# A decoder block whose engine queues are sorted by the scheduler's timeline simulation

## The chip, the cores and the metric

The kernel runs on one core of a Trainium2 chip. A core has five engines, each with a queue of its own that is fixed when the program is built: TensorE (PE; its weight loads are shown apart, as PEld), VectorE (DVE), ScalarE (ACT), GpSimd (POOL) and SyncE (SP), which issues most of the transfers between HBM and the on-chip memory. Engines wait for one another through semaphores. The metric is the time of one execution on the device in microseconds (us); for each kernel the median of several runs is given.

## The reference

One layer on 512 tokens of width 1024, all in float32:

```
mod = silu(c) @ w_ada + b_ada        # shift, scale, gate for both halves
h = rmsnorm(x) * (1 + scale1) + shift1
x_rnn, q_lat, kv_lat, k_rope, g_rnn, g_mla = split(h @ w_in)
xc = causal_dwconv(x_rnn)            # 4 taps, 1280 channels
y_rnn = rg_lru(xc)                   # two gates, a linear recurrence over tokens
q, k, v = ...                        # 16 heads from the two latents, rotary part
y_mla = causal softmax attention     # 16 heads, 64 + 32 wide
merged = sigmoid(g_rnn) * (y_rnn @ w_proj_rnn) + sigmoid(g_mla) * (y_mla @ w_proj_mla)
x = x + gate1 * (merged @ w_out)
h2 = rmsnorm(x) * (1 + scale2) + shift2
u = causal_dwconv(h2 @ w_up)         # 3 taps, 2 x 2816 channels
x = x + gate2 * ((silu(u_gate) * u_val) @ w_down)
return rmsnorm(x)
```

## The kernel before

Activations stand with channels on the 128 partitions and the 512 tokens along the free axis, so that most products give a 128x512 tile in one PSUM bank. A float32 product is made of three matmuls in a reduced format: each operand is split in a high part (ACT, L133) and a low part (DVE, L134), and high times high, high times low and low times high are summed in PSUM (L165 to L167; in the token-major products L704 to L706). A weight is loaded by a transfer of 512 KB into one of three buffers called raw (L154), split into one of two buffers each of whl and whg, and used by TensorE; so every weight passes through a transfer, ACT and DVE before TensorE can take it, and a raw buffer comes free when DVE has split it.

The eight PSUM banks are shared out by tag: tr has three, acc three, fil and gm one each. The stages are:

- Start: x is loaded, its row sums of squares are taken, the modulation vectors of the first half are computed on DVE (L327), x is transposed (L351) and scaled to h, called A in the trace, and the latents for attention are projected.
- Attention, 16 heads: a head's scores go to the three acc banks (L573 to L575); DVE adds the mask and takes the maximum (L578), ACT takes the exponential (L585), TensorE transposes the result P (L595) into tr banks, ACT and DVE split it as pt, and TensorE multiplies it by V (L608). The projections of q, k and v for the next heads use the bank fil (evacuated at L516/L517 and L559/L560; the rotary step is L487 to L498). Between these stand the projections for the two output gates, which have long been ready to run and are given a low priority, as filling (function fill); their bank is mostly gm. DVE also computes the second half's modulation here (L629).
- Recurrence, ten tiles of 128 channels: projection into a tr bank, convolution (L724, L726), two gate products into acc banks, a chain of some twelve steps on ACT and DVE (L734 to L746), the scan over tokens (L747), and the split into yr. At its start DVE normalises the attention output Y (L770) and splits it as yhl. Eight projections of the attention output (L779), which use the banks fil and gm, fill in.
- Merge: the recurrence output is projected (eight tiles, ten chunks each, tr banks), gated and split again.
- Out stage: the product with w_out, token-major. Its first half of the channels goes to four banks at once; the second half is done for one tile of 128 tokens after another, t = 0 to 3, in the banks gm, fil, gm, fil. For each tile DVE multiplies by the gate and adds the residual (L822, L823), ACT sums the squares (L855), a few one-column steps give the norm's factor (L225 to L233), DVE scales the tile as R (L857), TensorE transposes it (L862), ACT and DVE apply scale and shift (L867, L869) and split it (L871, L872) as A, the input of the FFN.
- FFN: 44 projections of eight chunks each, the convolution (L898, L900), the gate, the product with w_down, the last norm and the output. Its first four weight tiles are split ahead into the ff and whl/whg buffers, and their products are done for the first 256 tokens ahead of the rest.

The order of the work is not written out. The kernel's functions issue instructions in program order, with priorities (tc.high_priority with an offset, such as AHR for the recurrence's projections or -LOW for the filling ones) and in some places a fixed chain (tc.issue_after, through in_order). From these, the dependencies and the buffers, the scheduler sets one static queue per engine when the program is built. The semaphores follow from the queues and the dependencies.

## Time and profile before

| | us |
|---|---|
| median of 3 runs | 892.94 (892.58 to 895.51) |
| the profiled execution | 893.23 |
| its span in the trace | 891.4 |

The profiled execution lies 0.3 us over the median, and 1.8 us of it lie outside the span. TensorE was granted 0.995 of its full clock. A row of a group or of the timeline names the line, engine and operation, then output<-inputs by the program's names; x is the count, the number in brackets the idle time before and what ended it. A matmul's end is modelled, and two that follow each other overlap in such rows.

### The profile page before, as it was taken

What the parts mean: (1) busy time and instruction counts of PE and PEld (TensorE: products, weight loads), DVE (VectorE), ACT (ScalarE), POOL (GpSimd) and SP (SyncE); (2) the same over time, 40 slices, a digit from 0 to 9 for tenths busy, and PEclk for the clock granted to TensorE, in tenths of its full rate; (3) what the DMA queues carried; (4) which work ended last, traced back from release to release, by engine and by line L of the source; (5) the groups of instructions that cost most, each with busy time, mean ns of one, the idle gap of its engine ahead of it and who ended that gap; (6) DMA issues with size and microseconds to landing.
All of it is one profiled execution on the core that took longest, in us unless ns stands there. A gap on an engine that the chain in (4) does not pass through costs nothing.

```text
span 891.4 us, 11238 instructions
## 1 busy us (share of the span) xinstructions
PE 861.5 (97%) x4032; PEld 688.9 (77%) x4032; DVE 644.7 (72%) x1222; ACT 487.7 (55%) x898; POOL 18.8 (2%) x43
## 2 busy tenths in 40 slices
PE   6999999999999999999999999999999999999996
PEld 2777877877877777777878898888788888788885
DVE  6988888879866989998655779766766666423524
ACT  4566777667745888888334545444544444322323
POOL 0001000001020000000000000000000000000000
PEclk9999999999999999999999999999999999999998
DMA  9903232334463243354325074333233233333322
GB/s 356 353 33 105 73 105 95 98 119 144 143 175 108 97 142 125 135 160 171 118 71 166 1 263 142 114 94 93 80 94 94 93 94 95 95 94 95 95 71 95
DMA packets 33804, 109.08 MB, mean 122 GB/s; under 512 B 4290, under 2 KB 8002, under 8 KB 33748
## 3 DMA queue, kind: packets, MB, share of 16 engines
q1 hardware_dynamic: 32116, 103.60, 35.2%
q0 software_dynamic: 1632, 4.75, 2.3%
q8 instruction: 32, 0.52, 0.2%
q14 instruction: 24, 0.20, 0.1%
HBM read 103.59 MB, written 2.13 MB: 119 GB/s over the span
## 4 chain that ended last, share of the span: by engine, by line
PE 62%; ACT 3%; DVE 3%; DMA 2%; issue 1%; POOL 0%; ACTq 0%; DVEq 0%; POOLq 0%
PE acc L165 9%; PE acc L167 9%; PE acc L166 9%; PE tr L165 3%; PE tr L167 3%; PE tr L166 3%; PE acc L704 2%; PE acc L706 2%; PE acc L705 2%; PE tr L948 2%; PE tr L947 2%; PE tr L946 2%; PE gm L165 1%; PE fil L705 1%; PE fil L706 1%; PE fil L704 1%
## 5 line engine op out<-in xcount | busy, mean ns | idle before, releaser
L134 DVE TENSOR_TENSOR whg<-raw,whg 128x512 fp32r<-128x512 f32 x119 | 81.6, 688 | 84.0 <-ACT whg L133 83.8
L133 ACT ACTIVATE whl<-raw 128x512 fp32r<-128x512 f32 (+2 forms) x131 | 74.8, 576 | 112.1 <-PE acc L167 26.7
L133 ACT ACTIVATE whg<-raw 128x512 fp32r<-128x512 f32 x119 | 74.3, 627 | 108.0 <-PE acc L167 53.9
L134 DVE TENSOR_TENSOR whl<-raw,whl 128x512 fp32r<-128x512 f32 (+2 forms) x131 | 80.8, 621 | 52.6 <-ACT whl L133 52.2
L165 PE MATMUL acc<-A,whl 128*128 128x512 f32 x184 | 73.3, 399 | 0.0
L167 PE MATMUL acc<-A,whl 128*128 128x512 f32 x184 | 72.9, 396 | 0.0
L166 PE MATMUL acc<-A,whl 128*128 128x512 f32 x184 | 72.5, 394 | 0.0
L167 PE MATMUL acc<-A,whg 128*128 128x512 f32 x176 | 70.2, 399 | 0.1
L165 PE MATMUL acc<-A,whg 128*128 128x512 f32 x176 | 70.0, 398 | 0.3 <-ACT whg L133 0.3
L166 PE MATMUL acc<-A,whg 128*128 128x512 f32 x176 | 69.2, 393 | 0.0
L900 DVE SCALAR_TENSOR_TENSOR Y<-acc,vec,Y 128x511 f32<-128x511 f32 x86 | 64.3, 748 | 1.3
L585 ACT ACTIVATE P<-P,mx,qsc 128x512 f32<-128x512 f32 (+1 forms) x64 | 41.3, 648 | 7.1 <-DVE mx L581 7.1
L165 PEld LDWEIGHTS acc<-A,whl 128*128 128x128 f32 x184 | 34.6, 188 | 8.6 <-issue 0.5
L166 PEld LDWEIGHTS acc<-A,whl 128*128 128x128 f32 x184 | 34.6, 188 | 8.3
L167 PEld LDWEIGHTS acc<-A,whl 128*128 128x128 f32 x184 | 34.5, 188 | 8.3
L165 PE MATMUL gm<-A,whg 128*128 128x512 f32 x96 | 38.9, 406 | 1.7 <-ACT R L408 1.2
L165 PEld LDWEIGHTS acc<-A,whg 128*128 128x128 f32 x176 | 33.0, 188 | 9.1 <-ACT whg L133 1.4
L167 PEld LDWEIGHTS acc<-A,whg 128*128 128x128 f32 x176 | 33.0, 188 | 8.8 <-DVE whg L134 0.7
L166 PEld LDWEIGHTS acc<-A,whg 128*128 128x128 f32 x176 | 33.0, 188 | 8.0
L167 PE MATMUL gm<-A,whg 128*128 128x512 f32 x96 | 38.6, 402 | 0.0
L166 PE MATMUL gm<-A,whg 128*128 128x512 f32 x96 | 38.1, 397 | 0.0
L898 ACT ACTIVATE Y<-acc,vec 128x512 f32<-128x512 f32 x43 | 32.9, 764 | 5.1 <-PE acc L167 5.1
(493 smaller groups left out, 2236.5 us busy)
## 6 DMA issues: line engine op xcount, KB each, us to landing
raw<-in_w_up SPq DMA_DIRECT2D x44, 512.0 KB, 3.5
raw<-in_w_dn SPq DMA_DIRECT2D x22, 512.0 KB, 3.5
wa<-in_w_adat SPq DMA_DIRECT2D x16, 512.0 KB, 9.0
raw<-in_w_adat SPq DMA_DIRECT2D x16, 512.0 KB, 3.3
raw<-in_w_xr SPq DMA_DIRECT2D x10, 512.0 KB, 4.1
raw<-in_w_pr SPq DMA_DIRECT2D x10, 512.0 KB, 3.7
raw<-in_w_gm SPq DMA_DIRECT2D x8, 512.0 KB, 5.5
raw<-in_w_gr SPq DMA_DIRECT2D x8, 512.0 KB, 4.1
```

The lines of the kernel that those rows point to most:

```text
L133: S.activation(h, src, AF.Copy)
L134: return V.tensor_tensor(dst[:, 1, lo_c:lo_c + n], src, h.bitcast(F32), SUB).ins
L165: PE.matmul(out, wh, x[:, 0, xs], start=start, stop=False)
L166: PE.matmul(out, wh, x[:, 1, xs], start=False, stop=False)
L167: return PE.matmul(out, wl, x[:, 0, xs], start=False, stop=stop).ins
L585: S.activation(pq, pq, AF.Exp, scale=qsc[:, qb:qb + 1], bias=mx[:, qb:qb + 1], accum_out=sm[:, qb:qb + 1])
L704: PE.matmul(out, lt[:, 0, s], w[:, 0, :], start=start, stop=False)
L705: PE.matmul(out, lt[:, 0, s], w[:, 1, :], start=False, stop=False)
L706: return PE.matmul(out, lt[:, 1, s], w[:, 0, :], start=False, stop=stop).ins
L898: S.activation(u, b, AF.Identity, scale=vc("fw", 2 * 2 * NF + cj), bias=vc("fb", cj))
L900: V.scalar_tensor_tensor(u[:, d:], b[:, :T - d], vc("fw", (2 - d) * 2 * NF + cj), u[:, d:], MUL, ADD)
L946: PE.matmul(b, lt[:, 0, s], w[:, 0, o:o + n], start=start, stop=False)
```

## The change

The tile scheduler is told to sort the engines' queues by a timeline simulation of its own in place of its default order:

```diff
-    with _tile.TileContext(nc) as tc:
+    with _tile.TileContext(nc, schedule_with_timeline_sim=True) as tc:
```

The instructions, their operands, the buffers and the priorities that the kernel asks for are the same; what differs is where each instruction stands in its engine's queue, and with it the waits. TensorE's, DVE's and ACT's queues differ from the start of the program to the end of the out stage; in the FFN they are almost the same. In SP's queue eight loads of the first modulation move behind six other loads, and a few loads change places later.

In the rows below, the names are those of the tiles (tag and a number), output<-inputs and the shape of the output, with xN for a repeated row.

The first place is DVE's queue at the end of the out stage. T_4227 holds the residual sums of token tiles 2 and 3, T_4226 those of tiles 0 and 1; gm_4541 and fil_4603 are the banks of tiles 2 and 3; R_4506 is the scaled tile 1, rs_4512 its factor; ff_* are split FFN weights. Before:

```order
L226 TENSOR_SCALAR rs_4510<-ssq_4508,s_4361 128x1
L227 RECIPROCAL rs_4512<-rs_4511 128x1
L229 SCALAR_TENSOR_TENSOR rs_4510<-rs_4510,rs_4512 128x1
L233 SCALAR_TENSOR_TENSOR rs_4512<-rs_4510,rs_4512 128x1
L857 TENSOR_SCALAR R_4506<-T_4226,rs_4512 128x1024
L822 TENSOR_TENSOR T_4227<-gm_4541,acc_2781 128x512
L823 TENSOR_TENSOR T_4227<-T_4227,Y_4221 128x512
```

With the change:

```order
L822 TENSOR_TENSOR T_4227<-fil_4603,acc_2781 128x512
L872 TENSOR_TENSOR A_4384<-R_4445,A_4384 128x4x128
L823 TENSOR_TENSOR T_4227<-T_4227,Y_4221 128x512
L872 TENSOR_TENSOR A_4384<-R_4445,A_4384 128x4x128
L227 RECIPROCAL rs_4512<-rs_4511 128x1
L823 TENSOR_TENSOR T_4227<-T_4227,Y_4221 128x512
L134 TENSOR_TENSOR ff_4675<-raw_4673,ff_4675 128x512
L134 TENSOR_TENSOR ff_4690<-raw_4673,ff_4690 128x512
L134 TENSOR_TENSOR ff_4707<-raw_4705,ff_4707 128x512
L134 TENSOR_TENSOR ff_4722<-raw_4705,ff_4722 128x512
L229 SCALAR_TENSOR_TENSOR rs_4510<-rs_4510,rs_4512 128x1
L134 TENSOR_TENSOR ff_4739<-raw_4737,ff_4739 128x512
```

One more ff split and the step L233 follow, and then L857, which writes R_4506. The scale of tile 1 has moved from ahead of the residual sum of tile 2 to behind those of tiles 2 and 3 and six weight splits.

The same place in ACT's queue, where rs_4511 is tile 1's root and tr_4519 holds its first four transposes. Before:

```order
L225 ACTIVATE rs_4511<-ssq_4508,s_4361 128x1
L867 ACTIVATE R_4507<-tr_4519,B_522,A_521 128x128 x4
L855 ACTIVATE R_4568,ssq_4570<-T_4227 128x512
L871 ACTIVATE A_4384<-R_4507 128x4x128 x2
L225 ACTIVATE rs_4573<-ssq_4570,s_4362 128x1
L133 ACTIVATE ff_4675<-raw_4673 128x512
```

With the change:

```order
L225 ACTIVATE rs_4511<-ssq_4508,s_4361 128x1
L133 ACTIVATE ff_4675<-raw_4673 128x512
L133 ACTIVATE ff_4690<-raw_4673 128x512
L133 ACTIVATE ff_4707<-raw_4705 128x512
L133 ACTIVATE ff_4722<-raw_4705 128x512
L133 ACTIVATE ff_4739<-raw_4737 128x512
L133 ACTIVATE ff_4754<-raw_4737 128x512
L133 ACTIVATE whl_4771<-raw_4769 128x512
L133 ACTIVATE whg_4786<-raw_4769 128x512
L133 ACTIVATE whl_4927<-raw_4925 128x512
L133 ACTIVATE whg_4930<-raw_4925 128x512
L867 ACTIVATE R_4507<-tr_4519,B_522,A_521 128x128 x4
```

Ten weight splits now stand ahead of the step that reads tile 1's transposes. In TensorE's queue those transposes (L862) follow the last matmul into fil_4603, and the FFN's first matmul follows them; before, they stood 22 matmuls ahead of the end of fil_4603.

The last place is TensorE's queue around an attention head with few other matmuls, P_1578 being its exponentials, pt_* their split transposes, v_* its V, fil_1634 a projection of k. Before:

```order
L595 MATMUL tr_1617<-ident,P_1578 128x128 x2
L165 MATMUL gm_1295<-A_89,whg_1298 128x512
L575 MATMUL acc_1693<-kt_737,q_1212 128x128
L165 MATMUL fil_1634<-kvn_727,whl_1637 128x512
L166 MATMUL fil_1634<-kvn_727,whl_1637 128x512
L167 MATMUL fil_1634<-kvn_727,whl_1637 128x512
L165 MATMUL fil_1634<-kvn_731,whl_1637 128x512
L166 MATMUL fil_1634<-kvn_731,whl_1637 128x512
L167 MATMUL fil_1634<-kvn_731,whl_1637 128x512
L608 MATMUL tr_1623<-pt_1602,v_1361 128x512 x2
```

With the change:

```order
L595 MATMUL tr_1601<-ident,P_1578 128x128 x4
L595 MATMUL tr_1609<-ident,P_1578 128x128 x4
L595 MATMUL tr_1617<-ident,P_1578 128x128 x2
L608 MATMUL tr_1623<-pt_1602,v_1361 128x512 x2
L608 MATMUL tr_1623<-pt_1610,v_1361 128x384 x2
L608 MATMUL tr_1623<-pt_1618,v_1362 128x256 x2
L608 MATMUL tr_1623<-pt_1610,v_1362 128x128 x2
```

The products with V follow the transposes directly; the other matmuls stand elsewhere, in longer runs into one bank.

## The prediction

> **What bounds the kernel now.** I read the page first, then the busy time by stage, then TensorE's waits. The page's head says that TensorE is the engine to watch, with VectorE next:

> ```profile
> span 891.4 us, 11238 instructions
> PE 861.5 (97%) x4032; PEld 688.9 (77%) x4032; DVE 644.7 (72%) x1222; ACT 487.7 (55%) x898; POOL 18.8 (2%) x43
> ```

> The share of 72% is an average over stages that differ. By stage (from the left: window, its length, then busy time of PE, PEld, DVE, ACT, POOL):

> ```profile
> core 0: us, PE busy (x) PEld busy (x) DVE busy (x) ACT busy (x) POOL busy (x), PEclk, DMA share, GB/s
> 95.00:255.00 160.00, 153.85 (x858) 126.97 (x857) 135.91 (x331) 114.80 (x274) 7.34 (x14) 1.00 0.36 113
> 255.00:425.00 170.00, 165.26 (x690) 125.77 (x689) 146.35 (x227) 128.59 (x196) 4.71 (x8) 1.00 0.44 141
> 425.00:536.00 111.00, 109.44 (x580) 92.26 (x579) 72.70 (x137) 49.13 (x98) 0.96 (x1) 1.00 0.38 126
> 536.00:891.40 355.40, 348.13 (x1558) 282.74 (x1557) 211.88 (x331) 141.00 (x236) 0.00 (x0) 0.99 0.31 95
> ```

> In attention (95 to 255 us) DVE is busy for 135.91 of 160 us, in the recurrence (255 to 425) for 146.35 of 170: 85 and 86%. There an order of DVE's queue that puts one item late has about 24 us of slack in a whole stage to make it good. In the FFN (from 536) DVE is at 60%, and the change hardly moves anything there. So only what lies before 536 us is at stake. Last, whom TensorE waits for (total, times, longest):

> ```profile
> PE tr L249 <- DVE crow L246: 3.9, 1, 3.9
> PE gm L257 <- POOL mask L198: 2.4, 1, 2.4
> PE gm L165 <- ACT R L408: 1.9, 2, 1.2
> PE tr L165 <- ACT q L133: 1.3, 1, 1.3
> PE acc L165 <- ACT A L871: 0.6, 1, 0.6
> PE tr L862 <- DVE R L857: 0.6, 1, 0.6
> ```

> Of these rows the first two are the start; I put all of TensorE's waits together at about 23 us, 8 of them in the first 15 us. This is what a better order could win at most: TensorE does the same matmuls in any order.

> **The change, part by part.** No instruction is added or removed; each engine's static queue is sorted anew. A queue runs in its order, so I cost the change by queues: for a piece of DVE's or ACT's new queue that begins with an instruction reading a PSUM bank which TensorE has just finished, and ends with one whose output TensorE needs next, I add up the durations of the piece and compare them with TensorE's matmuls between the two. What is over is a hole in TensorE. The work of a DVE instruction counts from start to start, some 0.07 us under its duration; a 128x512 matmul counts 0.23 us, since pairs start that far apart while each lasts 0.39.

> *Out stage, t = 1.* The scale that makes R_4506 (L857) is moved behind the residual sum of the last tile, fil_4603, which TensorE completes only with the last matmul of the stage. The rows of before for what now lies between:

> ```profile
> 508.43 0.75 DVE L857 TENSOR_SCALAR R<-T,rs 128x1024 f32<-128x1024 f32 x1
> 509.24 0.69 DVE L822 TENSOR_TENSOR T<-fil,acc 128x512 f32<-128x512 f32 x1
> 509.85 1.89 DVE L134 TENSOR_TENSOR ff<-raw,ff 128x512 fp32r<-128x512 f32 x3
> 515.34 0.68 DVE L872 TENSOR_TENSOR A<-R,A 128x512 fp32r<-128x512 f32 x1
> 515.94 0.68 DVE L823 TENSOR_TENSOR T<-T,Y 128x512 f32<-128x512 f32 x1
> ```

> From start to start 509.24 to 509.85 is 0.61 and 515.34 to 515.94 is 0.60. The new piece of DVE's queue, with L822 of gm_4541, which can itself only start a matmul earlier, is 2 L822, 2 L872, 2 L823 and 6 splits: 12 x 0.61 = 7.3, with L857 (0.75) and three one-column steps (about 0.3) 8.4 us. TensorE has one thing left meanwhile: the transposes of that R. It stands still for 8.4 us.

> Then ACT: the shift and scale of those transposes (L867) now stand behind ten weight splits. The last four read two transfers whose buffers come free only when DVE has split their former content, 4.9 and 6.1 us into the hole.

> ```profile
> raw<-in_w_up SPq DMA_DIRECT2D x44, 512.0 KB, 3.5
> 515.36 0.63 ACT L133 ACTIVATE whl<-raw 128x512 fp32r<-128x512 f32 x1 [0.48 <-DMA raw<-in_w_up]
> 521.96 1.50 ACT L867 ACTIVATE R<-tr,B,A 128x128 f32<-128x128 f32 x4 [2.65 <-PE tr L862]
> 523.50 1.15 ACT L871 ACTIVATE A<-R 128x512 fp32r<-128x512 f32 x2
> 524.18 0.62 PE L165 MATMUL acc<-A,ff 128*128 128x256 f32 x3 [0.62 <-ACT A L871]
> 521.29 1.07 PE L862 MATMUL tr<-ident,R 128*128 128x128 f32 x8 [0.59 <-DVE R L857]
> ```

> The second lands at 6.1 + 3.5 = 9.6; two splits (1.2) make 10.8, L867 12.3, an L855 of about 0.6 that now stands between 12.9, and half of L871 13.5. In these 13.5 us TensorE does the transposes, 1.07. **+12.4 us**; 11 if the splits of DVE start before the bank is read, 14 if a transfer takes a microsecond more.

> *The last recurrence tile (yr_3797).* Before, TensorE had matmuls of the MLA projection to do while the chain of this tile ran:

> ```profile
> 407.24 0.39 PE L167 MATMUL acc<-xh,whl 128*128 128x512 f32 x1
> 408.23 0.69 ACT L734 ACTIVATE pr<-acc,hba 128x512 f32<-128x512 f32 x1
> 414.53 1.28 ACT L743 ACT_TABLE_LOAD   x1
> 418.01 1.22 DVE L747 TENSOR_TENSOR_SCAN pr<-pr 128x512 f32<-128x512 f32 x1
> 419.27 0.63 ACT L133 ACTIVATE yr<-pr 128x512 fp32r<-128x512 f32 x1 [0.60 <-DVE pr L747]
> 419.96 0.73 PE L165 MATMUL tr<-yr,whl 128*128 128x512 f32 x2
> ```

> The gates end at 407.6, the split is there at 419.9: 12.3 us, some of it other work between. Bare, the chain is ten dependent steps of about 0.7 with the scan, the split and what the table load adds: 9.3. Now 19 matmuls stand between the last gate and the first use, 19 x 0.23 = 4.4, with the gate's own end 4.7. **+4.7 us**; 3.5 at 8.2 for the chain without the table load, 7.6 with the 12.3 of before.

> *Attention.* The filling gate projections now come in blocks of up to 24 matmuls, where they were strewn between the steps of a head, so that a head's scores, transposes and products with V follow one another with less between. And on DVE, several instructions of other heads now stand between a score bank and the split that its product waits for. The dearest piece begins with the maximum over acc_2021 and ends with the split of pt_2191. Its members by these rows:

> ```profile
> L578 DVE CUSTOM_DVE_ANT_0 P<-acc,mask 128x512 f32<-128x512 f32 x16 | 11.0, 686 | 0.2 <-PE acc L575 0.2
> L629 DVE CUSTOM_DVE_ANT_0 raw<-raw,crow,vec 128x1024 f32<-128x1024 f32 x16 | 20.5, 1281 | 2.8 <-DMA raw<-in_w_adat 2.8
> L517 DVE TENSOR_TENSOR q<-fil,q 64x512 fp32r<-64x512 f32 x16 | 11.0, 687 | 1.2 <-ACT q L516 1.0
> L134 DVE TENSOR_TENSOR pt<-tr,pt 128x512 fp32r<-128x512 f32 x32 | 20.9, 684 | 2.9 <-ACT pt L133 2.6
> ```

> Two L629 at 1.21, sixteen of full size at 0.61 (two L578, four L517, four pt, the five of the rotary step, L613), and nine narrower ones, 2.7 together: 14.9 us, say 15, against 8.6 us of matmuls: 6.4 over. Seven more pieces that don't overlap give 2.5, 1.2, 0.3, 1.6, 1.0, 3.0 and 2.5: 18.6 in all. The same reckoning on the old queues gives 7.9 here, 4.0 in the recurrence and 0.5 in the out stage, 12.4 together, where the trace has about 15 us of waits outside the start. So the reckoning is near, and low if anything. **Net +10.7 us** (half to one and a half times that).

> *Recurrence.* The worst piece stands at its start: from the first convolution step on tr_2804 to the low split of whl_2979, 29 DVE instructions, among them eight normalisations of Y and eight splits of the result:

> ```profile
> L770 DVE TENSOR_TENSOR Y<-Y,yr 128x512 f32<-128x512 f32 x8 | 5.2, 686 | 3.2 <-DMA yr<-rd 3.2
> L134 DVE TENSOR_TENSOR yhl<-Y,yhl 128x512 fp32r<-128x512 f32 x8 | 5.2, 688 | 0.3
> ```

> 29 at 0.61 are 17.7 us, against 43 matmuls, 9.9 us: 7.7 over. Before, all sixteen stand ahead of that first convolution step. Six further pieces give 3.6, 0.5, 2.5, 1.5, 1.3 and 0.5: 17.6 in all, less the 4.0 of before. **Net +13.6 us**, with the same bounds as in attention.

> *Start.* In SP's queue eight modulation loads (512 KB each) move behind cst, posi, three loads of w_gm and vec1. The transfers run close together here, and the matmuls that follow the latents are ready at about the same time: **+0.6 us**, from -0.9 to 2.1. On POOL only two memsets change places, before any use: nothing, and hidden under the loads of x.

> *The clock.* Where TensorE was idle for long, its next matmuls ran slowly. At the start, by rows:

> ```profile
> 8.38 3.78 PE L249 MATMUL tr<-crow,ones 128*128 128x512 f32 x4 [3.91 <-DVE crow L246]
> 18.46 3.17 PE L257 MATMUL gm<-mask,ones 128*128 128x512 f32 x6
> ```

> Four of one form take 0.95 each after the idle time, six of the same form 0.53 each when it has been working: 4 x 0.42 = 1.7 us per long hole. The out stage has two long holes (8.4, then about 4): **+3 us**; none at all is the lower end, five holes (8.5) the upper.

> [...]

> Sum: 12.4 + 4.7 + 10.7 + 13.6 + 0.6 + 3 = 45.0. The profiled execution took 893.23 us, 0.3 over the median, so **938 us** against 892.94.

> **The rivals.**

> *Only the two fixed holes* (12.4, 4.7) and the start. For it: in attention and recurrence DVE is idle for 24 us each, and could run ahead into TensorE's blocks of fill. Against it: the reckoning found the waits of before about right. 893.2 + 17.7 = 911 us.

> *More than I add up.* Each weight split that is late also frees its load buffer late, of which there are three, and the next transfer needs 3.5 us. If nine of the pieces that end in a weight split each brought one such transfer into view, 9 x 3.5 = 31: about 969 us. Against it: the DMA share of 0.36 and 0.44 leaves the transfers short.

> *Not slower.* The blocks of fill could keep TensorE fed past what it waits for now; the first wait, 3.9 on crow, may also shrink, since that product now stands ahead of the sums of squares on DVE. If all 23 us went, and of the new costs only the lower ends of the two fixed holes came (11 + 3.5), 893.2 - 23 + 14.5 = 885 us. It decides only if attention and recurrence cost nothing, and the hole after fil_4603 can't be escaped by any engine's running ahead, since it begins with TensorE's own last matmul. If the gain came to 15 it would be no change.

> **How the numbers follow.** My forecast has 0.75, the two holes alone 0.12, more than I add up 0.08, not slower 0.05 (faster 0.03, within 0.3% 0.02; 0.3%, 2.7 us, is about what a measurement of this kernel can tell from none). The forecast's own range, from the lower ends 11 + 3.5 + 12.2 - 0.9 = 25.8 to the upper ends 14 + 7.6 + 36.5 + 2.1 + 8.5 = 68.7, is 919 to 962; to hold eight in ten it reaches down towards the two holes alone: **910 to 962 us**. Slower: 0.75 + 0.12 + 0.08 = 0.95.

> **What would show it.** In the changed profile TensorE should wait for "DVE R L857" once for about 8 us and then for "ACT A L871" for about 4, around the end of the out stage; wait about 5 us for the split of yr; show waits of several us for DVE's pt, whl and whg splits between 95 and 430 us; and the stretch of the FFN should be as long as it was, 355 us. TensorE's busy time should hardly change. If the out stage has no such pair of waits, the queue argument is wrong; if it has, and the stages before are as long as they were, DVE ran ahead.

## The result and the profile after

The changed kernel takes 977.82 us (median; 976.90 to 982.99), the kernel before, timed beside it, 893.13 us: a ratio of 1.0955, with a 95% interval of 1.0912 to 1.0997. It is slower by 84.7 us, as forecast in sign, and by nearly twice the forecast 45; 977.82 lies outside 910 to 962. The profiled execution is the slowest of the four, 982.99 us, 5.2 over the median. One of the three executions of the kernel busy_after below ran at a lower granted clock than the others and took longer (1039.0 us at 0.838, the others 981.08 and 980.12 at 0.983 and 0.982), and is compared with nothing.

The head of the page of the changed kernel, to be laid beside the one of before:

```profile
span 981.2 us, 11235 instructions
PE 886.5 (90%) x4032; PEld 714.1 (73%) x4032; DVE 647.3 (66%) x1222; ACT 489.3 (50%) x898; POOL 18.7 (2%) x43
```

DVE and ACT do what they did, within 3 us. TensorE, with the same 4032 matmuls, is busy for 25.0 us more, and idle for 94.7 us instead of 29.9. The 89.8 us of the span are these two: 65 of waiting and 25 of slower matmuls.

Where they lie, by windows that end with the last product of attention with V, the last scan, and the start of the first FFN matmul. Before:

```profile
0.00:251.40 251.40, 236.30 (x1197) 186.40 (x1198) 212.34 (x528) 166.85 (x364) 12.61 (x33) 0.99 0.44 148
251.40:418.00 166.60, 161.02 (x676) 123.08 (x676) 141.20 (x219) 127.82 (x195) 5.20 (x9) 1.00 0.43 140
418.00:510.20 92.20, 91.47 (x405) 72.85 (x403) 58.35 (x106) 37.52 (x76) 0.00 (x0) 1.00 0.28 90
510.20:891.40 381.20, 372.73 (x1760) 306.60 (x1758) 232.76 (x370) 155.56 (x264) 0.96 (x1) 0.99 0.34 105
```

With the change (columns as in the prediction: window, length, busy time and count of PE, PEld, DVE, ACT, POOL, then the granted clock):

```profile
0.00:311.30 311.30, 270.84 (x1310) 217.94 (x1310) 219.60 (x539) 176.44 (x380) 12.57 (x33) 0.95 0.38 128
311.30:489.70 178.40, 149.49 (x573) 112.86 (x571) 137.78 (x211) 120.61 (x181) 5.19 (x9) 0.92 0.38 118
489.70:595.10 105.40, 90.01 (x386) 72.83 (x386) 60.86 (x107) 39.49 (x79) 0.95 (x1) 0.92 0.31 97
595.10:981.20 386.10, 376.12 (x1766) 310.52 (x1766) 229.10 (x365) 152.79 (x259) 0.00 (x0) 0.99 0.31 98
```

The lengths can't be subtracted as they stand, since matmuls have moved between the stages: 113 more are done by the end of attention, 103 fewer in the recurrence. At 0.23 us each:

| stage | longer by | matmuls moved in | lost |
|---|---|---|---|
| start and attention | 59.9 | +113, 26.0 us | 33.9 |
| recurrence | 11.8 | -103, -23.7 us | 35.5 |
| merge and out stage | 13.2 | -19, -4.4 us | 17.6 |
| FFN to the end | 4.9 | +6, 1.4 us | 3.5 |

They add up to 90.5 for 89.8. Attention has lost three times the 11.3 that the prediction gave it with the start, the recurrence twice its 18.3 (with yr), and the out stage about what it was given (15.4): 2.0 of its 17.6 are the end of the wait for yr, which falls into that window.

Whom TensorE waits for now:

```profile
PE tr L165 <- ACT whl L133: 18.4, 10, 3.1
PE tr L608 <- DVE pt L134: 9.2, 5, 3.7
PE tr L862 <- DVE R L857: 8.3, 1, 8.3
PE acc L165 <- ACT A L871: 7.0, 2, 5.2
PE tr L165 <- ACT yr L133: 5.1, 1, 5.1
PE tr L595 <- ACT P L585: 5.0, 3, 2.0
PE acc L165 <- ACT A L355: 4.5, 1, 4.5
```

Two of these rows before, where there is none for pt over 0.5:

```profile
PE tr L165 <- ACT whl L133: 1.1, 3, 0.5
PE tr L595 <- ACT P L585: 0.9, 3, 0.4
```

The rows of R, A and yr are the holes that the prediction named one by one. The largest is one that it did not have as a row of its own: ten waits of 0.7 to 3.1 us for the high split of a weight, on ACT, nine of them in the recurrence's projections. None of the waits in attention and recurrence, apart from that for yr, is longer than 3.7, so the single holes of 6.4 and 7.7 us that the prediction gave to these stages did not come as holes. The three named holes in TensorE's timeline:

```profile
491.66 1.22 PE L165 MATMUL tr<-yr,whl 128*128 128x512 f32 x2 [5.11 <-ACT yr L133]
...
588.04 1.94 PE L862 MATMUL tr<-ident,R 128*128 128x128 f32 x8 [8.31 <-DVE R L857]
595.14 1.01 PE L165 MATMUL acc<-A,ff 128*128 128x256 f32 x3 [5.16 <-ACT A L871]
```

And what stands behind one of the ten. The chain of waits of the changed kernel between 333 and 353 us (start, length, what; a piece that begins where the one above ends was released by it; pieces of 0.02 us between them, called issue, are left out):

```profile
333.89 3.49 DMA raw<-in_w_pm
337.40 0.64 ACT whg L133
338.06 1.29 DVE whg L134 x2
...
340.05 0.63 ACT xh L133
...
343.38 0.69 DVE pr L745
344.07 0.61 DVE whl L134
344.70 3.29 DMA raw<-in_w_ada
348.02 1.42 DVE acc L423 x2
349.43 0.67 DVE Y L737
350.13 0.73 ACT Y L738
...
352.22 0.53 ACT whl L133
352.79 0.80 PE tr L165
```

For 19 us TensorE is not in the chain at all. It goes from a transfer to ACT, to DVE, to ACT, back to DVE, which frees a load buffer (L134); into that buffer goes a transfer for the vector of the first gate (L419); its accumulation on DVE (L423) stands in the queue ahead of a step of the gates (L737), ACT's step after it stands ahead of the split of whl, and TensorE waits 3.11 us for that. No piece of one queue between two events of TensorE holds this sum.

### The profile page after: what moved, and what is told of

The parts are those of the page before. It is cut to its first block, busy times and chain, and to the rows that moved or that the text cites. A ratio compares the mean times of both kernels' runs of the same rounds, so it can differ in the third digit from the quotient of the medians.

```text
span 981.2 us, 11235 instructions
## 1 busy us (share of the span) xinstructions
PE 886.5 (90%) x4032; PEld 714.1 (73%) x4032; DVE 647.3 (66%) x1222; ACT 489.3 (50%) x898; POOL 18.7 (2%) x43
## 4 chain that ended last, share of the span: by engine, by line
PE 61%; DVE 11%; DMA 7%; ACT 7%; issue 2%; POOL 0%; DVEq 0%; ACTq 0%
PE acc L167 8%; PE acc L165 8%; PE acc L166 8%; PE tr L165 3%; PE tr L166 2%; PE tr L167 2%; PE acc L704 2%; PE acc L706 2%; PE acc L705 2%; DMA raw<-in_w_pm 2%; DMA raw<-in_w_adat 2%; PE fil L165 2%; PE tr L948 2%; PE tr L947 2%; PE tr L946 2%
## 5 line engine op out<-in xcount | busy, mean ns | idle before, releaser
L134 DVE TENSOR_TENSOR whg<-raw,whg 128x512 fp32r<-128x512 f32 x119 | 81.3, 689 | 102.7 <-ACT whg L133 102.5
L133 ACT ACTIVATE whl<-raw 128x512 fp32r<-128x512 f32 (+2 forms) x131 | 75.2, 575 | 131.3 <-issue 29.5
L133 ACT ACTIVATE whg<-raw 128x512 fp32r<-128x512 f32 x119 | 73.7, 628 | 124.1 <-PE acc L167 60.9
L134 DVE TENSOR_TENSOR whl<-raw,whl 128x512 fp32r<-128x512 f32 (+2 forms) x131 | 81.2, 621 | 52.2 <-ACT whl L133 51.9
L165 PE MATMUL acc<-A,whl 128*128 128x512 f32 x184 | 71.5, 399 | 5.4 <-ACT A L355 4.5
L167 PE MATMUL acc<-A,whl 128*128 128x512 f32 x184 | 73.8, 401 | 0.0
L167 PE MATMUL acc<-A,whg 128*128 128x512 f32 x176 | 70.1, 398 | 0.0
L165 PE MATMUL acc<-A,whg 128*128 128x512 f32 x176 | 69.4, 395 | 0.0
L900 DVE SCALAR_TENSOR_TENSOR Y<-acc,vec,Y 128x511 f32<-128x511 f32 (+1 forms) x86 | 64.1, 748 | 1.3
L165 PE MATMUL tr<-A,whl 128*128 128x512 f32 x80 | 35.1, 439 | 15.6 <-ACT whl L133 15.6
L165 PEld LDWEIGHTS acc<-A,whl 128*128 128x128 f32 x184 | 34.7, 190 | 14.0 <-ACT A L355 4.7
L165 PE MATMUL gm<-A,whg 128*128 128x512 f32 x96 | 39.0, 406 | 2.2 <-ACT whg L133 2.2
L167 PEld LDWEIGHTS acc<-A,whl 128*128 128x128 f32 x184 | 34.9, 190 | 7.9
L578 DVE CUSTOM_DVE_ANT_0 P<-acc,mask 128x256 f32<-128x256 f32 (+1 forms) x64 | 28.8, 484 | 17.9 <-PE acc L575 17.7
L165 PEld LDWEIGHTS acc<-A,whg 128*128 128x128 f32 x176 | 33.0, 188 | 8.2 <-issue 0.2
L167 PE MATMUL tr<-A,whl 128*128 128x512 f32 x80 | 35.1, 439 | 4.0 <-DVE whl L134 4.0
L167 PEld LDWEIGHTS acc<-A,whg 128*128 128x128 f32 x176 | 33.0, 188 | 7.7
## 6 DMA issues: line engine op xcount, KB each, us to landing
raw<-in_w_up SPq DMA_DIRECT2D x44, 512.0 KB, 3.5
raw<-in_w_dn SPq DMA_DIRECT2D x22, 512.0 KB, 3.6
wa<-in_w_adat SPq DMA_DIRECT2D x16, 512.0 KB, 9.0
raw<-in_w_adat SPq DMA_DIRECT2D x16, 512.0 KB, 3.2
raw<-in_w_xr SPq DMA_DIRECT2D x10, 512.0 KB, 3.5
raw<-in_w_pr SPq DMA_DIRECT2D x10, 512.0 KB, 3.5
raw<-in_w_gm SPq DMA_DIRECT2D x8, 512.0 KB, 5.2
raw<-in_w_gr SPq DMA_DIRECT2D x8, 512.0 KB, 3.8
```

Of the source, the lines that this page charges most:

```text
L133: S.activation(h, src, AF.Copy)
L134: return V.tensor_tensor(dst[:, 1, lo_c:lo_c + n], src, h.bitcast(F32), SUB).ins
L165: PE.matmul(out, wh, x[:, 0, xs], start=start, stop=False)
L167: return PE.matmul(out, wl, x[:, 0, xs], start=False, stop=stop).ins
L578: V.tensor_tensor_reduce(out=pt[:, POFF[qd]:POFF[qd] + n], in0=sc[qd], in1=mask[:, T - n:], scale=1.0, scalar=-3e38, op0=ADD, op1=ALU.max, ...
L900: V.scalar_tensor_tensor(u[:, d:], b[:, :T - d], vc("fw", (2 - d) * 2 * NF + cj), u[:, d:], MUL, ADD)
```

## The experiments

All kernels but the plain two are built with queues that are imposed: a table for an engine lists its instructions, and each is told to be issued behind the one ahead of it in the table. Such a link sets an order and adds no wait. An engine without a table is sorted by the default order around those that have one. The edit that all of them share:

```diff
+QUEUES = {'PE': ..., 'DVE': ..., 'Activation': ..., 'Pool': ..., 'SP': ...}
+def _queues(tc, nc, *engines):
+    traced = list(nc.cur_bb.bb.instructions)
+    for engine in engines:
+        q = ...
+        for i, j in zip(q[:-1], q[1:]):
+            tc.add_manual_dep(traced[j], traced[i].name, mybir.DependencyInfo(mybir.DependencyClass.NoSync, ...), reason="queue")
...
+        _queues(tc, nc, *QUEUES)
```

The whole tables of either kernel give that kernel's queues row by row. The diffs below show only what else differs. Each ratio is against the kernel before, on the same chip.

| kernel | us | ratio and interval | us over before |
|---|---|---|---|
| the change | 977.82 | 1.0955 (1.0912 to 1.0997) | 85 |
| busy_after | 981.08 | 1.0988 (1.0954 to 1.1022) | 88 |
| out_as_before | 962.34 | 1.0773 (1.0737 to 1.0810) | 70 |
| out_only | 908.07 | 1.0181 (1.0146 to 1.0215) | 16 |
| att_only | 950.65 | 1.0642 (1.0609 to 1.0676) | 59 |
| rnn_only | 929.53 | 1.0410 (1.0381 to 1.0440) | 38 |
| noload_after | 966.42 | 1.0839 (1.0790 to 1.0887) | 74 |
| noload_before | 889.30 | 0.9963 (0.9953 to 0.9973) | -3 |
| nomod_after | 961.73 | 1.0769 (1.0748 to 1.0791) | 69 |
| nomod_before | 888.35 | 0.9954 (0.9926 to 0.9983) | -5 |
| pe_only | 974.82 | 1.0916 (1.0873 to 1.0959) | 82 |
| dve_only | 1025.00 | 1.1478 (1.1448 to 1.1508) | 132 |
| dve_act_only | 1028.57 | 1.1528 (1.1494 to 1.1563) | 137 |
| fills_spread | 939.96 | 1.0538 (1.0489 to 1.0587) | 46 |
| heads_order | 917.99 | 1.0273 (1.0237 to 1.0310) | 24 |

### Is it the clock?

The mean granted clock fell from 0.995 to 0.954, and TensorE's busy time rose by 25 us. If that were on the path, filling the holes with idle work would give a part of it back. busy_after has all queues of the change, and 63 matmuls with zero weights in 16 of the longest holes:

```diff
+IDLE = {514: 5, 528: 4, 567: 2, ..., 1688: 12, 1712: 7}
+    def busy(out, start):
+        hook[0] += 1
+        n = out.shape[-1]
+        EXTRA.append([PE.matmul(out, mask[:, :P], mask[:, :n], start=start, stop=start).ins
+                      for _ in range(IDLE.get(hook[0], 0))])
...
+        busy(out, start)
         PE.matmul(out, wh, x[:, 0, xs], start=start, stop=False)
```

> The queues of the change, written out as a table and imposed, with 63 extra matmuls on TensorE (a zero weight, so they add nothing) placed in 16 of the holes that the changed kernel's trace shows, 60 to 70% of each hole's length, just ahead of the matmul that waits. Theory clock: about 20 to 25 us of the 85 are matmuls run at half clock after windows in which TensorE was busy for less than half of 3.4 us; with the holes filled the granted clock rises from 0.954 to 0.975 or more and the time falls by 8 to 18 us, to 960 to 970. Rival: the slow matmuls lie beside other waits and cost nothing; the time stays within 3 us of 978 or grows by up to 10.

Measured: 981.08 us at a granted clock of 0.983. Seven tenths of what the clock had lost are back (0.954 to 0.983, of 0.995), and no time is: the interval of the ratio overlaps that of the change. The likely reading is that most of the slow matmuls lie ahead of waits that end when another engine is done, where a faster matmul only waits longer. What the 63 matmuls cost where a hole had already closed is in the same number, at most 63 x 0.23 = 14.5 us, so a gain of some 12 us could be hidden; one of 17, seven tenths of 25, could not.

### Which stage?

out_only takes the order of the out stage and what follows from the change, all else from before; out_as_before is its counterpart. att_only and rnn_only take that of start and attention, and of the recurrence, from the change.

```diff
-QUEUES = {'PE': <the change's>, ...}
+QUEUES = {'PE': <before's, with the out stage's places filled in the change's order>, ...}      # out_only
+QUEUES = {'PE': <the change's, with the out stage's places filled in before's order>, ...}      # out_as_before
+QUEUES = {'PE0': <up to the end of attention, the change's>, 'PE1': <the rest, before's>, ...}  # att_only
+QUEUES = {'PE0': <attention, before's>, 'PE1': <recurrence, the change's>, 'PE2': <rest>, ...}  # rnn_only
```

> Only the out stage and the FFN in the order of the change, the rest exactly as before. The prediction's terms: 12.4 and about 3.4 for the clock over before, to about 908.5; the changed kernel without its out stage gave back 15.5 (977.8 to 962.3). If the three stages alone add up to less than 70, they make one another worse.

> The queues of the change imposed, except that all instructions of the out stage and the FFN stand among themselves in the order of before. Theory queues, by the prediction's out-stage term and the clock of two long holes: the time falls by 12.4 + 3.4, to about 962. Rival: the holes only hide other waits, which come up when they go; it falls by less than 6, to 972 or more.

> Start and attention (with the gate projections) in the order of the change, recurrence, merge, out stage and FFN in the order of before, each stage's order imposed on each engine and the default scheduler left to interleave the two. Theory queue sums, by the prediction's terms: 10.7 + 0.6 over before, to about 904. Rival, from the changed kernel's trace (25 us more TensorE idle time up to the end of attention, and half clock besides): 25 to 45 us over before, 918 to 938.

> Only the recurrence and merge in the order of the change, the rest as before, imposed in the same way. Theory queue sums: 13.6 + 4.7 over before, to about 911. Rival, from the changed trace (23 us more TensorE idle time there, and half clock besides): 23 to 35 us over before, 916 to 928.

Measured: out_only costs 16.1 us (908.07 - 891.96), as the prediction's terms say (908.5), and its waits are those that the queue sums named:

```profile
PE tr L862 <- DVE R L857: 8.3, 1, 8.3
PE acc L165 <- ACT A L871: 5.6, 2, 3.7
```

out_as_before gives back as much: 1.0955 - 1.0773 is 0.018, 16 us. The prediction had 12.4 for the stage and 3 for the clock after it, 15.4: this term was right. The 3.4 for the clock in two of the expectations is twice the 1.7 us a hole from the start's rows, not rounded.

att_only costs 58.7 us, more than either expectation, but its queues don't fit together where the two orders meet, just behind the attention:

```profile
PE tr L165 <- ACT whl L133: 19.9, 5, 16.6
```

Taking off that one wait of 16.6, which the change doesn't have, leaves 42 us. rnn_only costs 37.6, just over its rival's range. The three stages make 42 + 37.6 + 16.1 = 95.7 for 85, so they are not quite separate; but each of the two long stages costs far more by itself than its term in the prediction (11.3 and 18.3). So the excess needs no interplay of stages.

### Is it the transfers, or the modulation on DVE?

The chain above passes through a load for the first gate, which has a low priority, and its accumulation. noload leaves out 24 such loads, 16 for the second half's shift and scale and 8 for the first gate (the steps work on data that is there instead, so these three vectors are not the reference's); nomod leaves out the steps L629 and the first gate's L423 as well, and GpSimd sets the shift and scale to zero. Both were made of the change's queues and of before's.

```diff
-                    w = raw()
-                    dma(w, a["w_adat"][2 * NK + NK * e + k])
+                    w = crow
...
-                            V.tensor_tensor_reduce(out=w[:, c], in0=w[:, c], in1=crow[:, c], scale=0.5,
+                            V.tensor_tensor_reduce(out=w[:, c], in0=w[:, c], in1=crow[:, c], scale=0.0,
...
-            r = alloc()
-            dma(r, a["w_ada2"][sec, kk])
+            if sec == 0:
+                r = h[:, 0].rearrange("p e n -> p (e n)").bitcast(F32)
+            else:
+                r = alloc()
+                dma(r, a["w_ada2"][sec, kk])
```

For nomod, the loops themselves are cut:

```diff
-                for i in range(2):
+                for i in range(2 * sec):
                     c = slice(i * T, i * T + T)
                     V.scalar_tensor_tensor(acc[:, c], r[:, c], cact[:, kk:kk + 1], acc[:, c], MUL, ADD)
...
-                    w = raw()
-                    ...
-                            V.tensor_tensor_reduce(out=w[:, c], in0=w[:, c], in1=crow[:, c], scale=0.5,
-                            ...
```

> The queues of the change imposed, with the 24 loads (512 KB each) of modulation weights in attention and recurrence left out: DVE does the same steps at the same places in its queue, on tiles that are there already (so these modulation vectors are wrong), and the three load buffers serve the other weights alone. Theory transfers: the waits that the queue sums missed come from loads brought into view by the three buffers, which those late DVE steps hold; the time falls by 20 us or more, to 957 or less. Rival queues: the engines' order alone makes the holes; it falls by 6 us at most, what DVE itself waits for these loads.

> The queues of before imposed, with the same 24 loads left out in the same way. Both theories: the loads are hidden there; the time falls by 4 us at most, to 889 or more. If it falls as far as with the queues of the change, the loads cost as much in either order and say nothing of the change.

> The queues of the change imposed, with the 24 modulation loads and also the 32 DVE steps that use them (16 of L629 in attention, 16 of L423 in the recurrence) left out; these modulation vectors are wrong. Theory misplaced low-priority work: such steps stand in DVE's queue ahead of steps that a head or a recurrence tile waits for, and hold everything behind them; without them the time falls well under the 966 that leaving out the loads alone gave, to 930 or less. Rival chains: the order of the critical steps themselves makes the holes, through DVE and ACT in turn; it falls to 945 to 960, about the steps' own 31 us of DVE work that the chains pass through in part.

> The queues of before with the same loads and steps left out. Both theories: they are hidden there; 3 to 6 us under before, 886 to 889.

What counts is the distance between the two orders. With everything it is 0.0955, 85 us. Without the loads it is 1.0839 - 0.9963 = 0.0876, 78 us; without the steps too, 1.0769 - 0.9954 = 0.0815, 73 us. The transfers are 7 us of the loss, the modulation's work on DVE some 5 more; the intervals of the ratios are 1 to 5 us to either side, so both are small and neither is sure to a few us. With all of it gone, six sevenths of the loss stand. From the change's own 978, noload_after takes off 11, between what its two theories asked for (20 or more, 6 or less), and nomod_after ends just above the 945 to 960 of "chains", far from the 930 of "misplaced low-priority work". So these transfers are links in chains that would be nearly as late without them. Loads of other weights use the same three buffers and are still there, but with the 24 gone ACT and DVE wait only 7.6 us in all for loads into raw in attention and recurrence (29.3 in the change, 12.3 before), and 78 of the 85 us stand all the same.

### Which engine's queue?

The prediction was made from DVE's and ACT's queues. pe_only imposes TensorE's queue of the change, dve_only DVE's, dve_act_only DVE's and ACT's; the default order sorts the other engines around it.

```diff
-QUEUES = {'PE': ..., 'DVE': ..., 'Activation': ..., 'Pool': ..., 'SP': ...}
+QUEUES = {'PE': ...}                      # pe_only
+QUEUES = {'DVE': ...}                     # dve_only
+QUEUES = {'DVE': ..., 'Activation': ...}  # dve_act_only
```

> TensorE's queue as in the change, all others left to the default scheduler. DVE's and ACT's queues alone as in the change gave 1028.6. Theory: TensorE's order is not what costs; with DVE and ACT sorted to suit it the time is nearer before than the change, under 930 (the out stage keeps part of its hole, since the transposes stand last there, about 3 to 8 us). Rival: either half of the change alone costs as much as both, 960 or more.

> DVE's queue alone as in the change. Theory chains through DVE and ACT in turn: with ACT free to follow, part of the loss goes, 930 to 970. Rival: DVE's order alone carries it all, 1000 or more, since ACT's steps follow DVE's anyway.

> DVE's and ACT's queues as in the change, TensorE's, SP's and GpSimd's left to the default scheduler, which sorts them around these. Theory: the holes come from what DVE and ACT do first, and TensorE's order only follows; the time is within 15 us of the changed kernel's 978. Rival: TensorE's blocks of fill make the holes, by taking away what covered a head's steps; the time is nearer before, under 930.

Measured: TensorE's queue alone brings 82 us, as much as the whole change; DVE's alone brings 132, and DVE's with ACT's 137, more than either expectation for it. The theory that DVE's and ACT's order is at fault, and TensorE's would do no harm under the default order of the others, has fallen. So has the reverse, that the default order of TensorE heals the loss. TensorE's queue or DVE's, imposed alone, costs as much or more. My reading, which these runs don't show by themselves, is that each is half of a plan, and that a sort that did not make the plan doesn't fit the other half to it as well. In these runs the other engines' queues are neither those of before nor those of the change, since they are sorted anew around the imposed one; one queue of the change with all others word for word as before wasn't tried.

With TensorE's queue imposed, the waits are of another make-up but the same size. In pe_only:

```profile
PE tr L595 <- ACT P L585: 18.0, 10, 4.5
PE tr L165 <- ACT whl L133: 13.0, 9, 2.9
```

### What in TensorE's queue?

Two things differ in it: the filling matmuls stand in blocks, and the steps of the heads (scores, transposes, products with V) stand in another order, two heads close behind each other. fills_spread is pe_only with the filling matmuls strewn as before (102 runs of them, half of three or fewer) and the out stage as before. heads_order is TensorE's queue of before with only the heads' steps in the change's order. With TensorE's queue of before imposed and nothing else, the sort gives all engines the queues of before, row by row; in heads_order DVE's and ACT's queues differ from those inside attention alone.

```diff
-QUEUES = {'PE': <the change's>}
+QUEUES = {'PE': <fills in before's places, the rest in the change's order, from the out stage on before's>}  # fills_spread
+QUEUES = {'PE': <before's, with L573 to L575, L595 and L608 in the change's order>}                          # heads_order
```

> TensorE's queue imposed, the other engines left to the default scheduler: all of TensorE's instructions up to the out stage in the order of the change among themselves, but the 576 matmuls of the filling projections (gates in attention, MLA projection in the recurrence) in the queue's places where the order of before has them (102 runs, half of them 3 or shorter, where the change has 60, half of them 10 or longer); the out stage as before. Theory cover: TensorE's order costs because the filling comes in blocks and leaves a head's or a tile's steps bare; spread again, the time is under 915. Rival: the order of the other matmuls costs; with the 5 to 10 us of the out stage gone from 974.8, the time is 945 or more.

> TensorE's queue as before, the other engines left to the default scheduler, but scores, transposes and products with V of the 16 heads in the order of the change among themselves (in the places that these steps have before). Theory cover: the order of the head steps themselves matters little; within 10 us of before, under 903. Rival: heads in pairs, as the change has them, cost; 915 or more.

Measured: heads_order costs 24 us, with the rest of TensorE's queue as before. The window to the end of its attention:

```profile
0.00:277.20 277.20, 244.81 (x1197) 194.50 (x1198) 213.75 (x528) 167.52 (x364) 12.59 (x33) 0.95 0.40 134
```

That is 25.8 us more than the 251.40 of before, with the same 1197 matmuls; in the recurrence it loses nothing (its last scan ends 166.5 us later, for 166.6). The mechanism shows in the timeline, at the second head of a pair:

```profile
214.80 0.69 DVE L578 CUSTOM_DVE_ANT_0 P<-acc,mask 128x512 f32<-128x512 f32 x1
...
220.88 0.45 PE L608 MATMUL tr<-pt,v 128*128 128x384 f32 x2
...
223.64 0.15 DVE L581 TENSOR_TENSOR mx<-mx,nqsc 128x4 f32<-128x4 f32 x1
223.82 0.81 ACT L585 ACTIVATE P<-P,mx,qsc 128x512 f32<-128x512 f32 x1 [1.27 <-DVE mx L581]
226.53 0.90 PE L595 MATMUL tr<-ident,P 128*128 128x128 f32 x3 [5.20 <-ACT P L585]
```

The same head before:

```profile
202.19 0.69 DVE L578 CUSTOM_DVE_ANT_0 P<-acc,mask 128x512 f32<-128x512 f32 x1
...
208.22 0.75 PE L608 MATMUL tr<-pt,v 128*128 128x384 f32 x5
...
211.58 0.15 DVE L581 TENSOR_TENSOR mx<-mx,nqsc 128x4 f32<-128x4 f32 x1
...
216.03 1.31 PE L595 MATMUL tr<-ident,P 128*128 128x128 f32 x10 [0.44 <-ACT P L585]
```

In heads_order the maximum over its scores is done at 215.4, and the small product that turns it into the exponential's bias (L581, four columns, 0.15 us long) comes at 223.6, behind thirteen other steps of DVE's queue: one of the modulation (L629), five of the rotary step for another head, the splits of the first head's pt, of two weights and of two pieces of k. Only then does ACT start on the exponentials, one block after another (2.5 us), and TensorE, which has reached the end of its matmuls ahead of the transposes at 221.3, stands for 5.20. Before, the path is no shorter: the product comes 8.8 us after the maximum, behind fourteen steps, and the transposes follow at 216.0. But there 32 matmuls (20 of projections, 12 of the next head's scores) stand between the first head's last product and these transposes, and TensorE waits for 0.44. In heads_order these 32 come after the first transposes. A head's path between its scores and its transposes goes through DVE, ACT and back, and needs TensorE to have other work meanwhile; what the new order takes away is not a short path but the work that covered it. With two heads close behind each other, the second has none.

The change itself takes away cover in the same way at another step. Its longest wait in attention is at the head of P_1578, where the products with V now follow the transposes directly and the split of pt stands behind other steps of DVE:

```profile
182.88 2.61 PE L608 MATMUL tr<-pt,v 128*128 128x512 f32 x8 [3.68 <-DVE pt L134]
```

fills_spread costs 46 us where pe_only costs 82. In the recurrence, pe_only first:

```profile
305.70:490.00 184.30, 150.85 (x573) 113.63 (x571) 137.84 (x212) 120.52 (x181) 5.16 (x9) 0.90 0.37 114
```

and fills_spread:

```profile
275.50:464.20 188.70, 167.35 (x681) 127.16 (x680) 143.82 (x220) 129.18 (x196) 5.20 (x9) 0.98 0.40 126
```

Worked out as in the table of stages, pe_only loses 184.3 - 166.6 + 103 x 0.23 = 41.4 us there, fills_spread 188.7 - 166.6 - 5 x 0.23 = 20.9. In attention it is 54.3 - 113 x 0.23 = 28.3 (end at 305.7) and 24.1 - 3 x 0.23 = 23.4 (end at 275.5). So strewing the fills gives 5 us in attention and 20 in the recurrence; the other 10 of the 36 lie behind it, where fills_spread has the out stage of before. Its 940 us lie between the two expectations (under 915, 945 or more). TensorE's waits in fills_spread:

```profile
PE tr L595 <- ACT P L585: 12.5, 7, 4.9
PE tr L165 <- ACT whl L133: 8.9, 9, 1.9
```

The waits for whl shrink from 13.0 to 8.9, those for P from 18.0 to 12.5. In pe_only, then, the heads' order, which costs 25.8 us in attention by itself, is about the size of what attention loses (28.3), and the blocks of fill make about half of what the recurrence loses. The change's own queues lose 33.9 and 35.5 there; that the same two causes share these losses in the same way is inferred, not shown. The other 21 us of the recurrence come with the order of the remaining matmuls or with how DVE and ACT are sorted around it; which, no run here tells.

## Why the prediction was wrong in size

**The out stage (12.4, and 3 for the clock): right.** The hole at R was 8.31 for 8.4 and that at A 5.16 for about 4 (3.7 in out_only), and the stage alone cost 16.1 for 15.4. The piece that the prediction summed begins with TensorE's own last matmul, TensorE has nothing else to do, and only one queue at a time lies between: what the sum assumes holds there.

**The last recurrence tile (4.7): right**, 5.11.

**Attention (+10.7) and the start (+0.6): mis-sized by a factor of three**, 33.9 in place of 11.3. The step that failed is "for a piece of DVE's or ACT's new queue that begins with an instruction reading a PSUM bank ... and ends with one whose output TensorE needs next, I add up the durations of the piece". Such a piece sees one engine's queue. A head's path is DVE, ACT, TensorE, ACT and DVE again: the 8.2 us from a maximum to its small product in heads_order end with something that ACT needs, not TensorE, so no piece of the sum holds them. The path was as long before (8.8 us) and cost 0.44, for 32 matmuls covered it. What the prediction had to price was the cover that goes; it noted that a head's steps follow one another "with less between", and gave that change no price of its own. And its dearest piece, 6.4 us over, did not come as a hole: the longest wait of the stage is 3.68. In the start, the row of "ACT A L355", 4.5 us, was not foreseen.

**Recurrence (+13.6, with yr 18.3): mis-sized by two**, 35.5. It is the same step of the prediction that failed. The largest piece was taken to be 7.7 us, at the stage's start; the waits there are 1.89 and 1.97. What came was ten waits for whl of up to 3.1 us; the one that was followed back, from 352.79 to 333.89, ends a path of more than a dozen steps over four queues. By fills_spread about half of such a loss comes with the blocks of fill; the cause of the rest stays open.

**The test of the reckoning did not test it.** The same sums on the old queues gave 12.4 for about 15, "So the reckoning is near, and low if anything". But in the old order the fills are strewn, and a path over several engines can be as long as 8.8 us and cost 0.44; that the sums were right there says nothing of an order in which the fills stand in blocks. "Half to one and a half times" was therefore no bound.

**"TensorE's busy time should hardly change": wrong**, by 25.0 us. The clock term of 3 was meant for two holes, and what TensorE lost to the clock is far more. But busy_after got seven tenths of the clock back and no time, and at most some 12 us can be hidden there, so the clock by itself did not make the forecast wrong.

**The rivals.** *Only the two fixed holes* (911) fell: attention and recurrence lost 69 us. Its reason may hold in part, since the largest single pieces did not come as holes. *More than I add up* (969) came nearest in size, with its chance of 0.08, but its mechanism, a late load buffer and a transfer of 3.5 us, is 7 us by noload for the 24 modulation loads, not 31, and little waiting for other loads is left there. *Not slower* fell; the gain at crow did come, since its wait of 3.9 is not among the large rows any more, but a new one for A (L355) is of the same size.

**The signs.** The pair of waits in the out stage, the wait for yr and those for DVE's pt (9.2 us in five) came; those in the recurrence were for ACT's split of whl (18.4) far more than for DVE's (4.0).

**The FFN as long as it was: nearly**, 386.1 for 381.2 us, 1.4 of it six matmuls more, and its first 6 us (595.1 to 601.3) at a granted clock of 0.50.

## What to carry to other kernels

An order of several queues is one plan: cost it by the path of one unit of work (a head, a tile) through all the engines, and ask at each step what TensorE has to do meanwhile; a sum over one engine's queue came out right here only where the queue starts from TensorE's own last result, and two to three times too low elsewhere. Filler that is strewn in small pieces hid such paths better than the same filler in blocks (20 us in one stage, 5 in another); of two units close behind each other, one found no cover. And a kernel's agreement with a reckoning before a change is no test of the reckoning if the change takes away the cover that made it agree.

## What the runs showed of the hardware

```profile
229.27:232.68 3.41, 2.19 (x13) 1.40 (x11) 3.38 (x12) 1.69 (x5) 0.00 (x0) 1.00 0.41 138
232.68:239.51 6.83, 5.02 (x14) 4.07 (x15) 3.69 (x11) 5.61 (x17) 0.00 (x0) 0.50 0.47 161
...
348.74:352.15 3.41, 0.94 (x5) 0.42 (x3) 2.29 (x5) 2.61 (x6) 0.00 (x0) 1.00 0.49 141
352.15:358.98 6.83, 6.19 (x15) 4.78 (x16) 6.22 (x11) 4.87 (x9) 0.00 (x0) 0.50 0.11 34
```

In the 3.41 us before a fall TensorE was idle only in part: it worked for 2.19 and 0.94 us of them here, and of the twelve only the one in the out stage's hole had no work at all. Ten of the twelve have less than half of the 3.41, two have more (1.81 and 2.19), so the "less than half of 3.4 us" in the expectation of busy_after fits most of the falls and not all. Nor did less than half always bring half clock: the window from 270.22 to 273.63 us has 1.60 us of work and full clock follows. How much work keeps the clock up, no run here settles. At half clock the matmuls start 0.43 us apart and not 0.23:

```profile
353.81 0.63 PE L167 MATMUL tr<-A,whl 128*128 128x512 f32 x1
354.23 0.63 PE L165 MATMUL tr<-A,whl 128*128 128x512 f32 x1
354.66 0.63 PE L166 MATMUL tr<-A,whl 128*128 128x512 f32 x1
```
